# Order edges at the up-projection and in attention of a hybrid decoder block

## The chip, the cores and the metric

The kernel runs on one NeuronCore of a Trainium2 chip. The metric is the device time of one execution in microseconds; a time stated for a kernel is the median of its runs. TensorE (PE in the profile) multiplies matrices, VectorE (DVE), ScalarE (ACT) and GpSimd (POOL) work element by element, and SyncE (SP) issues most of the transfers. Each engine works through its own list of instructions in order.

## The reference

One decoder layer on `x` of 2048 tokens by 1024 channels, all in float32:

```python
h = rmsnorm(x, attn_norm);  z = h @ w_in          # pool | q | k | v | gate_pool | gate_attn
a = pool_mixer(u_pool, w_pool, pool_scale)        # 4 groups, causal means over 2, 4, 8, 16 tokens, minus u
q, k = rope(rmsnorm(q)) / 8, rope(rmsnorm(k))     # 16 query heads, 2 key heads of 64
b = sliding_window_attention(q, k, v, sinks)      # window 128, blocks of 128
x = x + (sigmoid(g_pool) * a + sigmoid(g_attn) * b) @ w_out
h = rmsnorm(x, ffn_norm)
up = causal_depthwise_conv(h @ w_up)              # width 3, 2 x 2816 channels
x = x + (silu(gate) * val) @ w_down
```

## The kernel before

Tokens go through in two chunks of 1024 (c = 0 and 1), channels on the partitions. Every float32 matrix product is made of three matmuls: each operand is split into a high part (a cast on ScalarE) and a low part (a subtraction on VectorE), and high x high, high x low and low x high are added up in PSUM. `split` (L249, L250), `halved` (L362, L363), `parted` (L1068, L1069) and `Down.make` (L1870, L1871) all do this: ScalarE's cast first, then VectorE's subtraction, and TensorE needs both.

A chunk has these stages. First the keys and values of eight blocks of 128 tokens, with query projections, and in chunk 0 the folding of `w_pool` into `w_in`, as fillers in between (`mixer`, first loop; L1939). Chunk 0 also takes its row norms here: `squares` (L683) sums the squares of one block of rows, which it loads first into a tile `M`, `norm1` makes the scale, `spread` (L666) turns it by transposes on TensorE.

Then attention, 32 items of four heads and one block (`mixer`, second loop; L1984). An item's `scores` makes the products, the masked maximum, the exponentials (L917) and the normalisation (L923); the next turn's `probabilities` transposes (L931), splits and masks (L939, on GpSimd) and `values` (L959) multiplies by the values. Between the items stand fillers: projections for queries, gates and pooled channels. What a filler leaves for the other engines is put in two lists. `later` holds the next slab's split, the gates' combination and the start of a pooling window; `run_later` empties it at every call. `slow` holds a window's doublings (L1015) and its end (`finish`: L1026, L1027, the store of `dd`); `run_later(n)` takes up to n of them. A window of 2, 4, 8 or 16 has 1, 2, 3 or 4 doublings. In the last group of chunk 0 the loop also calls `w.step` of gate units, which split their weights piece by piece (`Blocks.first` to `fourth`).

Then the gates, the output projection (`out_proj` in chunk 0, `out_blocks` with seven products in chunk 1), the up-projection (`up`) and the down-projection (`Down`). The gates, chunk 1's output projection, the up- and the down-projection use Strassen's scheme in Winograd's form, seven products of half-size blocks where eight would do, with sums on VectorE before and after. In `up`, a unit f is one tile of gate and value channels; its products `one` to `seven` each run 12 matmuls (`product`, L1254) into one PSUM bank. `three` adds to the bank that `one` began, and `kept` (L1444) copies it away on ScalarE; then `five` adds to that same bank (L1470 takes its result), and then `seven` (L1478). `four` and `six` share another bank. The first three units are interleaved by hand while the right-hand sums T1 to T4 are being made (`right_t1` to `right_t4`).

In `out_blocks`, `final` adds the residual (`added`, L1320), squares the result on ScalarE (L1332, L1335) and adds the square to a running sum (L1339); `stats` turns the sums into row scales with matmuls against ones (L655).

In `Down`, each step of the seven products has its operand made up to five steps ahead (`AHEAD`); at `P2` the step first makes a difference in place (L1888).

The order on each engine isn't the program's order. A planner (the tile framework's scheduler) walks the program once at build time, keeps a list of instructions by priority (the order in which they are traced), and with its own table of costs picks for each engine the first that it thinks ready; it also hands out the buffers of each pool then (`U` 19, `M` 5, `F` 4, `R` 3, `Q` 6). On the chip the order is fixed. `tc.issue_after(ins)` adds an order edge, without a wait: what the block traces on the engine of `ins` is planned behind `ins`. On other engines it does nothing.

Of the kernel before, what the change touches and what calls it, by code (L numbers as in the profile page):

```python
# [21 lines left out]
ALU = mybir.AluOpType  # L22
# [200 lines left out]
def block_kernel(ctx: ExitStack, tc: tile.TileContext, x, xT, pos, vec, qkn, w_poolT, w_pool, w_q, w_kv,  # L223
# [753 lines left out]
    def run_later(n=2, after=None):  # L977
        while later:
            later.pop(0)()

        with tc.issue_after(after) if after else nullcontext():
            for _ in range(min(n, len(slow))):
                slow.pop(0)()

    def gate_attn(c, ct, n, hs, ta, st):
# [22 lines left out]
    def windows(c, ct, u, st):  # L1008
# [20 lines left out]

        slow.append(finish)  # L1030

    def gated(c, ct, n, hs, ta, st):
# [217 lines left out]
    def product(bank, a, b, first):  # L1250
        i = 0
        for k in range(4):
            for x, y in ((0, 0), (0, 1), (1, 0)):
                nc.tensor.matmul(bank, a[:, x, k, :], b[k // 2][:, y, k % 2, :],  # L1254
                                 start=(first and i == 0), stop=(i == 11),
                                 skip_group_check=True)
                i += 1

    class Out:


        def __init__(self, c):
            self.c, self.m, self.w, self.b, self.xs, self.raws = c, [], [], {}, {}, []
            self.accs = [[], []]

        def mix(self):
# [51 lines left out]
        def added(self, h, n, m, bank):  # L1318
            x = self.xs[h, n][:, m]
            V.scalar_tensor_tensor(x, bank, 0.5, x, op0=ALU.mult, op1=ALU.add)  # L1320

# [4 lines left out]
        def final(self, h, n, m, bank):  # L1326
            self.added(h, n, m, bank)
            x = self.xs[h, n][:, m]
# [4 lines left out]
            else:  # L1333
                sq = mp.tile([P, 512], F32, "M")
                A.square(sq, x)  # L1335
                if h == 1 - n == 0 and m == 3:
                    accs.append(sq)
                else:
                    V.tensor_add(accs[0], accs[0], sq)  # L1339
            A.dma_start(x2d[4 * h + m][:, n * 512:n * 512 + 512], x)  # L1340
# [5 lines left out]
    def out_blocks(ob):  # L1346
# [52 lines left out]

        def stats(n):  # L1400
            rstd(ob.accs[n], r2[:, 4 * n:4 * n + 4])

# [30 lines left out]
    class Up:  # L1433
# [5 lines left out]
        def mul(self, bank, x, y, first=False):  # L1439
            product(bank, self.w.w[x], self.b[y], first)  # L1440

# [57 lines left out]
        def gate(self, yg=None):  # L1499
# [3 lines left out]
            A.activation(t, yg, AF.Silu)  # L1503
            V.tensor_mul(t, t, self.yv)
            load(actd[self.f], t)

    def up(c, xg, b, norms, heads, dn):
# [36 lines left out]
        with tc.issue_after(last):  # L1544
            right_b22(xg, b)
        u0.five()
        with tc.issue_after(third):
            right_t4(xg, b, t2s)
        weights(2, 1)
        u0.six()  # L1550
        yg = u0.conv(0, u0.ug)
# [6 lines left out]
        for f in range(2, FT + 1):  # L1558
# [24 lines left out]
            weights(f + 1, 1)  # L1583
            old.six()
            if f < FT - 1:
# [208 lines left out]
    class Down:  # L1794
# [80 lines left out]
        def run(self, extra):  # L1875

            gives = []
            for i, (g, p, k) in enumerate(self.steps):
# [7 lines left out]
                if p == "P2":  # L1886
                    a = self.raw[g, 0, k]
                    V.tensor_sub(a[:, 0:4:2], a[:, 1:4:2], a[:, 0:4:2])  # L1888
                if k > 0 and gives:
# [41 lines left out]
    def mixer(c, hs, kvw):  # L1931
# [7 lines left out]
        for n in range(NB):  # L1939
# [4 lines left out]
            if c == 0 and n == 3:  # L1944
                make_h(0, 2, hs)
                for i in range(4, NB):
                    squares(0, i, row(0, i))
            pk = [raw(0), raw(1)] if n == 0 else pk[1:] + ([raw(n + 1)] if n + 1 < NB else [])
# [11 lines left out]
            for f in fills:  # L1960
                filler(*f, c, hs, ta, st)
            next(parts, None)
            if n > 1 or n == c == 1:
# [20 lines left out]
        for i in range(len(items)):  # L1984
# [18 lines left out]
            if group == 3:  # L2003
                if c == 0:
                    if n == 0:
                        older = []
                        stream.fetch(stream.used + 2)
                    for f, steps in enumerate(({1: 1, 2: 2, 3: 1, 4: 0, 5: 0}, {5: 1, 7: 1})):
                        if n in steps:
# [137 lines left out]
```

## Time and profile before

| what | value |
|---|---|
| median of 3 runs | 2384.95 us (2383.26 to 2388.49) |
| the profiled execution | 2385.3 us |
| its span, first to last instruction | 2383.6 us |
| TensorE busy | 2356.7 us, 99% |
| VectorE / ScalarE / GpSimd busy | 1906.5 / 1185.7 / 190.5 us |
| mean granted TensorE clock | 0.998 |

A row of the groups reads: line, engine, operation, result from operands by tile names, shape, count, then busy time, mean of one in ns, and the idle time of the engine ahead of them with what ended it. A row of the timeline reads: start, length, engine, line, operation, tiles, shape, count, and in brackets the idle time ahead of it with what ended it. A row of the windows reads: stretch, its length, then for each engine busy time and instructions, the granted clock, the share of DMA time and GB/s.

### The profile page before, as it was taken

The page shows a single profiled execution, that of the slowest core. Times are in us where ns is not written, and L with a number is a line of the kernel's source. Part 1 is how long each engine was busy: PE and PEld are TensorE (multiplying, and loading weights), DVE is VectorE, ACT ScalarE, POOL GpSimd, SP SyncE. Part 2 cuts the span into 40 slices and gives each one's busy share as a digit, 9 for nine tenths or more (in the row PEclk, how much of TensorE's full clock was granted, in tenths as well). Part 3 has the DMA queues.
Part 4 walks back from the last instruction along what each step waited for, and adds up shares of the span by engine and source line. Part 5 has one row for each costly group of instructions (what it writes and reads, how often), then busy time and mean ns, then how long its engine had stood idle before and what let it go on. Part 6 is the DMA issues. An engine that isn't in the chain of part 4 may idle for free.

```text
span 2383.6 us, 30120 instructions
## 1 busy us (share of the span) xinstructions
PE 2356.7 (99%) x11040; PEld 1958.7 (82%) x11040; DVE 1906.5 (80%) x2907; ACT 1185.7 (50%) x2164; POOL 190.5 (8%) x142
## 2 busy tenths in 40 slices
PE   9999999999999999999999999999999999999999
PEld 8888888888788888888888888888788888888887
DVE  8688888977977777899955867788798777779994
ACT  7555455455654555643623544455445545554441
POOL 1123121010000000000002232200000000000000
PEclk9999999999999999999999999999999999999999
DMA  9768778697222233644454776666733222228421
GB/s 348 241 202 237 223 213 286 216 344 270 73 88 91 93 106 106 210 168 162 133 195 151 228 219 196 197 207 230 234 129 105 80 80 80 80 75 288 141 71 53
DMA packets 165060, 408.10 MB, mean 171 GB/s; under 512 B 14128, under 2 KB 50480, under 8 KB 155184
## 3 DMA queue, kind: packets, MB, share of 16 engines
q1 hardware_dynamic: 151616, 373.48, 46.6%
q0 software_dynamic: 8256, 24.12, 4.3%
q10 hardware_dynamic: 5040, 8.58, 1.0%
q8 instruction: 87, 1.43, 0.2%
q14 instruction: 61, 0.50, 0.1%
HBM read 267.32 MB, written 138.81 MB: 170 GB/s over the span
## 4 chain that ended last, share of the span: by engine, by line
PE 85%; DVE 8%; DMA 3%; ACT 2%; issue 1%; POOL 0%; SPq 0%; DVEq 0%; ACTq 0%; POOLq 0%
PE f L1254 22%; PE f L266 16%; PE t L1254 12%; PE a L1254 6%; PE f L1912 4%; PE a L1912 4%; PE s L1912 4%; PE t L1912 4%; PE f L1098 3%; PE a L959 2%; PE s L898 2%; PE a L266 2%; PE t L931 1%; DVE U L1069 1%; DMA U<-xd 1%
## 5 line engine op out<-in xcount | busy, mean ns | idle before, releaser
L266 PE MATMUL f<-U,U 128*128 128x512 f32 (+1 forms) x2088 | 490.2, 389 | 4.5 <-ACT U L249 2.1
L266 PEld LDWEIGHTS f<-U,U 128*128 128x128 f32 x2088 | 381.3, 189 | 81.3 <-ACT U L249 2.7
L1254 PE MATMUL f<-U,U 128*128 128x512 f32 x1872 | 445.1, 390 | 2.7 <-ACT Q L1444 2.5
L1254 PEld LDWEIGHTS f<-U,U 128*128 128x128 f32 x1872 | 350.8, 188 | 77.7 <-ACT Q L1444 3.8
L1492 DVE SCALAR_TENSOR_TENSOR M<-F,vc,M 128x1024 f32<-128x1024 f32 x176 | 225.3, 1282 | 139.0 <-ACT M L1489 138.7
L1254 PE MATMUL t<-U,U 128*128 128x512 f32 x1332 | 314.6, 389 | 0.0
L1254 PEld LDWEIGHTS t<-U,U 128*128 128x128 f32 x1332 | 249.7, 188 | 52.4 <-ACT Q L1444 0.3
L362 ACT CAST U<-R 128x1024 fp32r<-128x1024 f32 x147 | 153.6, 1053 | 82.0 <-DVE R L391 42.6
L1254 PE MATMUL a<-U,U 128*128 128x512 f32 x756 | 183.9, 390 | 0.7 <-ACT Q L1444 0.7
L363 DVE TENSOR_TENSOR U<-R,U 128x1024 fp32r<-128x1024 f32 x147 | 179.2, 1221 | 0.3 <-ACT U L362 0.3
L1254 PEld LDWEIGHTS a<-U,U 128*128 128x128 f32 x756 | 141.3, 188 | 30.2 <-ACT Q L1444 1.2
L1254 PE MATMUL f<-U,M 128*128 128x512 f32 x624 | 150.2, 389 | 0.3 <-DVE F L1470 0.3
L917 ACT ACTIVATE Q<-s,st,rq 128x128 f32<-128x128 f32 x256 | 113.8, 456 | 49.9 <-DVE st L914 49.7
L1254 PEld LDWEIGHTS f<-U,M 128*128 128x128 f32 x624 | 117.0, 188 | 25.0 <-DVE F L1470 0.8
L939 POOL TENSOR_SCALAR_AFFINE_SELECT M<-M 128x1024 fp32r<-128x1024 f32 x64 | 94.4, 1475 | 383.4 <-DVE st L919 230.4
L1870 ACT CAST U<-U 128x1024 fp32r<-128x1024 f32 x76 | 79.0, 1051 | 84.7 <-PE s L1912 22.2
L1478 ACT COPY F<-f 128x512 f32<-128x512 f32 x52 | 30.5, 586 | 182.2 <-PE f L1254 182.0
L1489 ACT ACTIVATE M<-F,vc 128x1024 f32<-128x1024 f32 x88 | 109.4, 1243 | 3.3 <-DVE F L1474 1.9
L1871 DVE TENSOR_TENSOR U<-U,U 128x1024 fp32r<-128x1024 f32 x76 | 92.0, 1219 | 2.7 <-ACT U L1870 2.5
L1870 ACT CAST F<-U 128x1024 fp32r<-128x1024 f32 x44 | 46.2, 1049 | 93.8 <-PE a L1912 62.5
L966 ACT COPY U<-a 128x512 f32<-128x512 f32 x64 | 37.5, 586 | 108.5 <-PE a L959 108.3
L1098 PE MATMUL f<-U,U 128*128 128x512 f32 x384 | 88.5, 390 | 0.3 <-DVE M L1104 0.2
(320 smaller groups left out, 4051.9 us busy)
## 6 DMA issues: line engine op xcount, KB each, us to landing
R<-w_up SPq DMA_DIRECT2D x80, 512.0 KB, 3.7
actd<-M SPq DMA_DIRECT2D x44, 512.0 KB, 2.7
U<-w_down SPq DMA_DIRECT2D x88, 256.0 KB, 5.0
U<-actd SPq DMA_DIRECT2D x88, 256.0 KB, 5.2
qd<-U SPq DMA_DIRECT2D x64, 256.0 KB, 3.8
Q<-qd SPq DMA_DIRECT2D x64, 256.0 KB, 4.7
R<-w_out SPq DMA_DIRECT2D x30, 512.0 KB, 4.5
U<-kept_S SPq DMA_DIRECT2D x12, 1024.0 KB, 7.9
```

Of the source, the lines that this page charges most:

```text
L266: nc.tensor.matmul(out, a, b, start=(i == 0), stop=(i == n - 1))
L362: A.copy(t[:, 0], raw)
L363: V.tensor_sub(t[:, 1], raw, t[:, 0].bitcast(F32))
L917: A.activation(pr[:, h, :], sc[:, h, 0:P], AF.Exp, bias=nm[:, h:h + 1], scale=it["rq"][:, h:h + 1], accum_out=rs[:, h:h + 1])
L939: G.affine_select(own.rearrange("p a h q -> p (a h) q"), pa.bitcast(F32).rearrange("p a h q -> p (a h) q"), pattern=[[0, 8], [1, P]], base ...
L1098: nc.tensor.matmul(po, w[:, a, k, :], ms[k // 2][n][:, b, k % 2, :], start=(first and i == 0), stop=(last and i + 1 == len(order)))
L1254: nc.tensor.matmul(bank, a[:, x, k, :], b[k // 2][:, y, k % 2, :], start=(first and i == 0), stop=(i == 11), skip_group_check=True)
L1489: A.activation(y, u[:, 2:], AF.Identity, bias=cw[:, 3, m:m + 1], scale=cw[:, 2, m:m + 1])
L1492: V.scalar_tensor_tensor(y, u[:, j:j + T], cw[:, j, m:m + 1], y, op0=ALU.mult, op1=ALU.add)
L1870: A.copy(hi, src)
L1871: V.tensor_sub(lo, src, hi.bitcast(F32))
L1912: nc.tensor.matmul(into[m], u[:, 0, c_], v[:, 1], start=(first and j == 0), stop=(k == n - 1 and j == 2), skip_group_check=True)
```

## The change

Nothing is added to or taken from what is computed; only order and edges change.

- `run_later(2)` takes one pooling step, not two, in a call by which a new window has been started (`fresh`) since the last such call.
- `product` returns its last matmul. In `up`, `u0.five` is planned behind the product traced before it (`u1.three`), `u0.six` behind `u0.five`, and `u1.six` (f = 2) behind `u0.six`. The weight step of unit 2 joins `right_t4` behind `third`, the last low part of T3, on VectorE.
- `final` puts the addition of a square to its sum in a list, and the next `final` traces it behind its own residual; `stats` empties the list.
- In `Down.run`, the difference of `P2` is planned behind the last product of gate and value (L1504).
- In `mixer`, chunk 0, block 3: the four `squares`, with the row loads they take, are traced behind that block's fillers.
- In the last attention group of chunk 0, third item, `run_later(0)` is called ahead of the weight steps.

```diff
@@ run_later
+        if n == 2 and run_later.fresh:
+            n, run_later.fresh = 1, False
         with tc.issue_after(after) if after else nullcontext():
             for _ in range(min(n, len(slow))):
                 slow.pop(0)()
+    run_later.fresh = False
@@ windows
         slow.append(finish)
+        run_later.fresh = True
@@ Out.final
-            self.added(h, n, m, bank)
+            with tc.issue_after(self.added(h, n, m, bank)):
+                while self.sums:
+                    self.sums.pop()()
...
-                    V.tensor_add(accs[0], accs[0], sq)
+                    self.sums.append(lambda: V.tensor_add(accs[0], accs[0], sq))
@@ out_blocks, stats
+            while ob.sums:
+                ob.sums.pop()()
@@ Up.mul, Up.gate
-            product(bank, self.w.w[x], self.b[y], first)
+            Up.end = product(bank, self.w.w[x], self.b[y], first)
...
-            V.tensor_mul(t, t, self.yv)
+            Up.gated = V.tensor_mul(t, t, self.yv).ins
@@ up
-        u0.five()
+        with tc.issue_after(Up.end):
+            u0.five()
         with tc.issue_after(third):
             right_t4(xg, b, t2s)
-        weights(2, 1)
-        u0.six()
+            weights(2, 1)
+        with tc.issue_after(Up.end):
+            u0.six()
+        six = Up.end
...
-            old.six()
+            with tc.issue_after(six) if f == 2 else nullcontext():
+                old.six()
@@ Down.run
-                    V.tensor_sub(a[:, 0:4:2], a[:, 1:4:2], a[:, 0:4:2])
+                    with tc.issue_after(Up.gated):
+                        V.tensor_sub(a[:, 0:4:2], a[:, 1:4:2], a[:, 0:4:2])
@@ mixer
                 make_h(0, 2, hs)
-                for i in range(4, NB):
-                    squares(0, i, row(0, i))
...
             for f in fills:
                 filler(*f, c, hs, ta, st)
+            if c == 0 and n == 3:
+                for i in range(4, NB):
+                    squares(0, i, row(0, i))
...
                         stream.fetch(stream.used + 2)
+                    if n == 2:
+                        run_later(0)
```

More of the change, by code (lines that the diff above doesn't have):

```diff
@@ L1253, in product @@
             for x, y in ((0, 0), (0, 1), (1, 0)):
-                nc.tensor.matmul(bank, a[:, x, k, :], b[k // 2][:, y, k % 2, :],
-                                 start=(first and i == 0), stop=(i == 11),
-                                 skip_group_check=True)
+                ins = nc.tensor.matmul(bank, a[:, x, k, :], b[k // 2][:, y, k % 2, :],
+                                       start=(first and i == 0), stop=(i == 11),
+                                       skip_group_check=True).ins
                 i += 1
+        return ins
     class Out:
@@ L1264, in __init__ @@
             self.accs = [[], []]
+            self.sums = []
         def mix(self):
@@ L1319, in added @@
             x = self.xs[h, n][:, m]
-            V.scalar_tensor_tensor(x, bank, 0.5, x, op0=ALU.mult, op1=ALU.add)
+            return V.scalar_tensor_tensor(x, bank, 0.5, x, op0=ALU.mult, op1=ALU.add).ins
         def residual(self, h, n):
```

## The prediction

> **What bounds the kernel now.** I read the page first, then what TensorE waited for, then the timeline at each of those waits, then windows for the granted clock. From the page: the busy line, one costly group and one DMA row.
>
> ```profile
> PE 2356.7 (99%) x11040; PEld 1958.7 (82%) x11040; DVE 1906.5 (80%) x2907; ACT 1185.7 (50%) x2164; POOL 190.5 (8%) x142
> L1254 PE MATMUL f<-U,U 128*128 128x512 f32 x1872 | 445.1, 390 | 2.7 <-ACT Q L1444 2.5
> U<-kept_S SPq DMA_DIRECT2D x12, 1024.0 KB, 7.9
> ```
>
> TensorE is busy 2356.7 of the span of 2383.6 us, and no edit removes or adds a matmul. Only the 26.9 us outside can be won, plus time lost to a lower clock. Who ended TensorE's waits (total us, times, longest):
>
> ```profile
> PE t L931 <- DVE Q L923: 4.1, 5, 1.4
> PE f L266 <- ACT U L249: 3.8, 5, 1.8
> PE f L1254 <- ACT Q L1444: 2.5, 2, 1.3
> PE a L655 <- DVE F L1339: 2.2, 1, 2.2
> ```
>
> These four rows are 12.6 of the 26.9 us, and each leads to lines that the diff reorders. Windows, with columns stretch, TensorE, weight loads, VectorE, ScalarE, GpSimd, clock, DMA:
>
> ```profile
> 353.50:357.10 3.60, 3.25 (x8) 2.61 (x9) 3.60 (x9) 2.20 (x10) 1.23 (x1) 0.53 0.83 261
> 608.20:611.80 3.60, 3.60 (x16) 2.97 (x17) 3.60 (x4) 2.90 (x3) 0.00 (x0) 1.00 0.02 5
> 1725.70:1729.20 3.50, 3.50 (x11) 2.61 (x10) 1.72 (x3) 0.63 (x1) 0.34 (x1) 0.51 0.97 298
> 1020.00:1080.00 60.00, 60.00 (x263) 49.14 (x263) 59.05 (x82) 24.90 (x30) 0.00 (x0) 1.00 0.47 161
> ```
>
> At full clock a matmul takes 3.60 / 16 = 0.225 us. At clock 0.53, eight took 3.25: 3.25 - 8 x 0.225 = 1.45 us lost, over and above the wait before them. The stretch at 1725.70, at 0.51, is as long, and I price it the same. The profile draws a matmul 0.39 us long but the next follows after 0.225, so each wait shown hides 0.16 more: a wait of w costs w + 0.16.
>
> **The up-projection's order (b).** Both chunks; first the weights' load and the waits in chunk 0, then in chunk 1:
>
> ```profile
> 595.74 0.32 SPq L243 DMA_DIRECT2D U<-kept_S  x1
> 607.56 0.58 ACT L1444 COPY Q<-f 128x512 f32<-128x512 f32 x1
> 608.20 3.04 PE L1254 MATMUL f<-U,U 128*128 128x512 f32 x12 [1.27 <-ACT Q L1444]
> 611.75 2.88 PE L1254 MATMUL f<-U,U 128*128 128x512 f32 x12
> 1760.58 0.32 SPq L243 DMA_DIRECT2D U<-kept_S  x1
> 1772.80 3.04 PE L1254 MATMUL f<-U,U 128*128 128x512 f32 x12 [1.27 <-ACT Q L1444]
> ```
>
> The product at 608.20 is `u0.five`: it accumulates into the bank that `kept` (L1444) is still copying, and TensorE stands still 1.27 us. `u1.three`, in another bank, was planned later, at 611.75. The new edge puts `u1.three` first: its 12 x 0.225 = 2.7 us of product cover the copy. Gain 1.27 + 0.16 = 1.43 a chunk, 2.9 in two. The cover fails if u1's weights S3/S2 are late, and `u0.five` is now queued behind them: each us late is a us lost. Issued at 595.74 with the median 7.9 us to landing they are there by 603.6, 3 us early; at 1760.58, 1768.5 against 1771.5. The edges on `u0.six` and `u1.six` keep products whole and cost nothing: the same matmuls follow. The weight step moved behind `third` delays VectorE work for unit 2 by about one subtraction; TensorE has units 0 and 1 in front of it. Bounds: 2.9 if both waits go, 1.4 if only one does. I take 2.9.
>
> **Sums behind the next residual (a).** Chunk 1's output projection:
>
> ```profile
> 1716.34 0.69 DVE L382 TENSOR_TENSOR R<-R,R 128x512 f32<-128x512 f32 x1 [4.71 <-DMA R<-w_up]
> 1717.26 4.24 PE L1298 MATMUL f<-U,U 128*128 128x512 f32 x18
> 1718.93 0.69 DVE L1339 TENSOR_TENSOR F<-F,M 128x512 f32<-128x512 f32 x1 [0.70 <-ACT M L1335]
> 1722.91 0.69 DVE L1339 TENSOR_TENSOR F<-F,M 128x512 f32<-128x512 f32 x1 [0.69 <-ACT M L1335]
> 1723.66 0.49 PE L655 MATMUL a<-one,F 128*128 128x1 f32 x3 [2.16 <-DVE F L1339]
> ```
>
> VectorE lost 4.71 us to the load of w_up, then ran residual, wait for ScalarE's square (0.70), sum, in rounds of (1722.91 - 1718.93) / 2 = 1.99. Without the wait a round is 1.29, or 0.645 an operation. After the change the sum of block m stands behind the residual of block m+1, when its square is long done. From 1716.34 + 0.65 come four residuals and four sums without idling, 8 x 0.645 = 5.2, ending at 1722.2; the fourth residual needs the first product of the row at 1717.26, done by 1717.26 + 2.7 = 1720.0, before its turn. So L655 starts at 1722.2, not 1723.66: 1.5 gained, and a wait of 0.7 stays. That is below the 1.27 of (b), after which the clock was 1.00 (row 608.20), so the 1.45 lost at 1725.70 goes too: 2.9. Bounds: 0.5 if the planner pulls another operation in between and the clock still drops; 2.16 + 0.16 + 1.45 = 3.8 if the wait vanishes. I take 2.9, by the counted operations. The sums hold their `M` tiles one block longer; the tile of block 3 of the first quarter is held through two products, with five `M` buffers, two of them temporaries. I cost that at nothing; the range of (a) covers it.
>
> **The split ahead of the weight steps (c).** Chunk 0, last attention group:
>
> ```profile
> 323.88 0.32 SPq L243 DMA_DIRECT2D R<-wfold  x1
> 349.03 0.69 ACT L1041 ACTIVATE F<-f,vc 128x512 f32<-128x512 f32 x1 [2.60 <-DVE f L1040]
> 350.22 1.04 ACT L362 CAST U<-R 128x1024 fp32r<-128x1024 f32 x1
> 351.17 1.14 ACT L249 CAST U<-R 128x512 fp32r<-128x512 f32 x2
> 351.84 1.19 PE L266 MATMUL f<-U,U 128*128 128x512 f32 x4 [1.79 <-ACT U L249]
> 353.85 6.74 PE L266 MATMUL f<-U,U 128*128 128x512 f32 x22 [0.51 <-DVE U L250]
> ```
>
> The next filler's slab was fetched at 323.88, yet its split (L249, L250) stands behind the weight step's cast (L362), and ScalarE idled 2.60 us before 349.03. `run_later(0)` traces the split first. If it fits into that idle stretch, both waits go with the clock drop: 1.79 + 0.16 + 0.51 + 0.16 + 1.45 = 4.1. If it only passes L362, it gains 1.04 and the clock may still drop: 1.0. The slab had 27 us to arrive, so I take 4.0. What is late instead are the steps of unit 0's weights, needed two fillers later.
>
> **Pooling steps one at a time (e).** Chunk 1's first item, then a collision in chunk 0:
>
> ```profile
> 1300.12 2.50 DVE L1015 TENSOR_TENSOR F<-F 128x1038 f32<-128x1038 f32 x2
> 1306.15 1.22 DVE L1015 TENSOR_TENSOR F<-F 128x1024 f32<-128x1024 f32 x1
> 1309.01 0.63 PE L931 MATMUL t<-identr,Q 128*128 128x128 f32 x4 [1.34 <-DVE Q L923]
> 336.63 2.10 POOL L939 TENSOR_SCALAR_AFFINE_SELECT M<-M 128x1024 fp32r<-128x1024 f32 x1 [5.97 <-DVE st L919]
> 337.69 2.11 DVE L1027 SCALAR_TENSOR_TENSOR F<-F,F 128x1024 f32<-128x1024 f32 x1
> ```
>
> With one doubling at 1300.12 instead of two the softmax chain behind it starts 1.25 earlier; the later slot holds as many as before. Of 1.34 I expect 1.0 back. At the four other waits of that row the doubling only changes its slot. Doublings, finish and the store of `dd` move one slot later; there are 28 steps a chunk against 32 slots of two, so none reaches the next stage. Bounds: all 4.1 of the row, and three new waits of its mean, 4.1 / 5 = 0.82, -2.5. I take 1.0. The last two rows speak against it: the finish took 2.11 beside a select of 2.10. The Trainium skill says why, in "SBUF — State Buffer", "Who interferes with whom": VectorE with two SBUF operands and a GpSimd instruction that reads SBUF lock each other out for a whole instruction. The trace agrees; by it a moved step that lands on a select makes both late, and (e) would be a loss.
>
> **Squares behind the fillers (f).** Chunk 0, block 3:
>
> ```profile
> 67.24 1.06 ACT L683 ACTIVATE M<-M 128x1024 f32<-128x1024 f32 x1
> 67.40 1.23 PE L266 MATMUL f<-M,U 128*128 128x256 f32 x6 [0.71 <-ACT U L249]
> 68.20 0.77 SPq L243 DMA_DIRECT2D M<-x  x1
> 68.30 0.61 ACT L249 CAST U<-R 128x512 fp32r<-128x512 f32 x1
> 73.68 1.06 ACT L683 ACTIVATE M<-M 128x1024 f32<-128x1024 f32 x1 [1.20 <-DMA M<-x]
> ```
>
> A square sits between the two casts that TensorE waits for: 0.71 + 0.16 can go, I take 0.8 and 1.2 at most, with the next cast. The moved step also issues four 512 KB row loads on SP, now planned behind the fillers' loads, and the fourth needs an `M` tile that a square frees. With the first square after the cast of 68.30 it is issued at 68.30 + 0.61 + 1.06 = 70.0, not 68.20; block 4's norm, and the transposes queued on TensorE, come 1.8 late: at worst 1.8 + 1.45 = -3.3. Query products stand ahead of them, which is why I take 0.8.
>
> **The difference at the down-projection (d).**
>
> ```profile
> 999.58 1.22 DVE L1888 TENSOR_TENSOR U<-U 128x1024 f32<-128x1024 f32 x1
> 1001.45 3.01 PE L1254 MATMUL f<-U,M 128*128 128x512 f32 x12 [0.35 <-DVE F L1470]
> ```
>
> L1888 stood in front of L1470; behind the last gate product it no longer does: 0.35 + 0.16 = 0.5. VectorE then has it in a stretch where it is busy 59.05 of 60 (row 1020.00), with operands made five steps ahead as cover; at worst as much is lost, -0.5.
>
> **Sum.** 2.9 + 2.9 + 4.0 + 1.0 + 0.8 + 0.5 = 12.1. Every edit also shifts the planner's list behind it; I allow one new wait of 0.82 a chunk, 1.6. That leaves 10.5. The profiled execution took 2385.3, 0.35 above the median of 2384.95: 2374.8 on its scale, 2374.5 as a median. All upper bounds, with no new wait, give 16.6 (2368.3); all lower ones, less the 1.6, give -5.0 (2390).
>
> **Rivals.** About 0.2%, 4.8 us, is what can be told from no change: 2380.2 to 2389.7.
> - *Waits change place.* Only (b), with fixed products, pays; (a), (c), (e) and (f) come back as waits on other lines, since the planner orders by its own costs: 2384.95 - 2.9 = 2382. For it: VectorE is 80% busy. Against: (c)'s operands were ready 27 us early.
> - *The clock does not come back.* The gaps shrink but the half-clock stretches stay: 2374.5 + 2 x 1.45 = 2377.4. Against: they follow exactly on the waits of 1.79 and 2.16, and none follows on the 1.27 of (b). (The Trainium skill, "TensorE: Matmul & The Clock Gate", "Why this matters for your kernels", lets the clock fall only for gaps over about 3 us; by that these waits would not be the cause. The trace, at 0.53 after 1.79 and 0.51, disagrees.)
> - *Slower: pooling steps on selects.* Each of the 32 attention items of a chunk has one select. A doubling or finish that meets it takes 2.11 - 1.22 = 0.9 longer, right ahead of L923, for which L931 waits. It decides from about 12 items (10.5 / 0.9); at 20 of them the time is 2374.5 + 18 = 2392.5. Now 5 of 64 wait, so this needs four times as many.
> - *More.* All five waits of L931 go and the allowance is not used: 2374.5 - 3.1 - 1.6 = 2369.8.
> - *The edges bind nothing*, because the planner already had this order: excluded by the rows 608.20 and 611.75.
>
> **Chances.** Forecast 0.60, waits change place 0.18, clock 0.06, more 0.10, slower 0.06. Faster by over 0.2%: 0.60 + 0.06 + 0.10 = 0.76, and 0.02 of the second case: 0.78. Within: 0.16. Slower: 0.06. The forecast's own range is 2371 to 2379; the one for 8 in 10 is 2368.5 to 2384, which reaches to the second case.
>
> **What would show it.** Right: no wait of L1254 on L1444 in `u0.five`; L655 waiting under 1 us and clock 1.00 behind it; L249 ahead of L362 and clock 1.00 around 350; L1888 behind the last L1504. Wrong: more than five waits of L931 on L923; a wait of `u1.three` on kept_S; a transposition L666 near 77 that waits for L683 or a row; a new window at half clock.

## Result: 18.7 us slower

The changed kernel takes 2403.19 us (median of 6 runs, 2401.17 to 2406.88) against 2384.46 for the kernel before beside it (6 runs, 2380.28 to 2388.49): the ratio is 1.0083, with a 95% interval of 1.0071 to 1.0095. The forecast was 2374.5, and its range ended at 2384.

The profiled execution took 2406.88 us, one of the two longest of the six, with a span of 2405.2. Line numbers of the changed kernel are a few higher: `product` is L1259, `kept` L1455, the sum behind `five` L1481, the cast and subtraction of `parted` L1073 and L1074, the residual L1327, the sum of squares L1348. The busy line of its page:

```profile
PE 2364.6 (98%) x11040; PEld 1963.7 (82%) x11040; DVE 1908.6 (79%) x2907; ACT 1185.5 (49%) x2164; POOL 199.7 (8%) x142
```

The counts are those of before (11040, 2907, 2164, 142): only order has changed. TensorE's busy time is 7.9 us longer, and 40.6 us of the span lie outside it, where it was 26.9. What ended TensorE's waits, the rows that bear on the change:

```profile
PE f L1259 <- DVE F L1481: 10.0, 4, 4.7
PE a L959 <- ACT M L933: 4.3, 1, 4.3
PE a L959 <- POOL M L939: 3.3, 4, 1.3
PE a L655 <- DVE F L1348: 2.0, 1, 2.0
PE t L931 <- DVE Q L923: 0.9, 2, 0.6
```

The waits that the prediction wanted gone are smaller (L923 was 4.1) or have other instances. New ones stand above them: the first row did not exist before beyond one wait of 0.35. The windows, cut where the clock changed (last columns: clock, DMA, GB/s):

```profile
86.43:89.84 3.41, 3.41 (x17) 3.41 (x17) 3.41 (x15) 0.79 (x2) 0.00 (x0) 0.50 0.06 26
393.63:397.04 3.41, 2.85 (x7) 2.25 (x8) 2.58 (x4) 3.41 (x5) 1.09 (x1) 0.50 1.02 404
632.56:639.38 6.82, 6.04 (x14) 4.79 (x15) 4.49 (x4) 4.87 (x8) 0.00 (x0) 0.50 0.00 0
1758.96:1765.78 6.82, 6.82 (x24) 5.95 (x24) 2.47 (x5) 1.26 (x3) 1.01 (x1) 0.50 0.89 310
1806.74:1810.16 3.42, 3.08 (x7) 2.51 (x8) 2.11 (x3) 3.36 (x4) 0.00 (x0) 0.50 0.00 0
```

Five stretches at half clock, 23.9 us in all, where before had two of 3.41. At a granted clock of 0.50 TensorE loses half of the time it works, so I estimate that a stretch of 3.41 or 6.82 us costs up to 1.7 or 3.4.

Where the time went, by stage. A stage ends where TensorE starts the first product of the next one; the numbers are differences from the profile of before, in us, and the stages left out differ by 0.03 at most. The last two columns are the experiments that split the change in two.

| stage | before | changed | `only_up` | `no_up` |
|---|---|---|---|---|
| start, keys and values, chunk 0 | 124.28 | +4.15 | +0.81 | +5.10 |
| attention, gates, output projection, chunk 0 | 455.15 | +0.89 | -0.37 | +2.81 |
| up-projection, chunk 0 | 424.87 | +7.99 | +9.52 | -0.71 |
| down-projection, chunk 0 | 212.61 | -1.19 | 0.00 | -1.18 |
| attention, chunk 1 | 263.95 | +1.19 | +1.79 | +1.41 |
| output and up-projection, chunk 1 | 505.25 | +8.12 | +0.72 | -3.94 |
| down-projection, chunk 1 | 211.27 | +0.53 | 0.00 | +0.54 |
| span | 2383.59 | +21.57 | +12.43 | +3.95 |

**How far such a table can be read.** One profile is one execution. Where an experiment leaves a stage's order as it was, the start came out between -0.1 and +1.6, attention to output projection of chunk 0 between -1.3 and +1.3, the up-projection of chunk 0 between -0.1 and +0.2, attention of chunk 1 between -0.2 and +0.3 but twice at +1.8 and +3.5, and output and up-projection of chunk 1 between -2.2 and +2.1. Nearly all of the last is the output projection (82.3 before): with VectorE's order there as before it took 77.9 to 84.4 in six kernels. From `up_fixed`:

```profile
1713.12 0.69 DVE L382 TENSOR_TENSOR R<-R,R 128x512 f32<-128x512 f32 x1 [0.40 <-DMA R<-w_up]
```

The load of `w_up`, for which VectorE waited 4.71 before, let it wait 0.40 in the profile of `up_fixed`, whose output projection has neither (a) nor another order on VectorE; it took 77.9, 4.3 less than before, and L655 did not wait. So a profile's gain of up to 4 us there can be the load's. The causes of the spread that I can see are transfers that land at another time, and whether a wait costs the clock. I call nothing an effect that lies within these ranges, and the medians decide.

### The profile page after: what moved, and what is told of

Read it like the earlier page. It is cut to its first block, busy times and chain, and to the rows that moved or that the text cites. A ratio compares the mean times of both kernels' runs of the same rounds, so it can differ in the third digit from the quotient of the medians.

```text
span 2405.2 us, 30132 instructions
## 1 busy us (share of the span) xinstructions
PE 2364.6 (98%) x11040; PEld 1963.7 (82%) x11040; DVE 1908.6 (79%) x2907; ACT 1185.5 (49%) x2164; POOL 199.7 (8%) x142
## 4 chain that ended last, share of the span: by engine, by line
PE 84%; DVE 8%; DMA 4%; ACT 2%; issue 1%; POOL 0%; DVEq 0%; SPq 0%; ACTq 0%; POOLq 0%
PE f L1259 21%; PE f L266 15%; PE t L1259 12%; PE a L1259 6%; PE f L1928 4%; PE a L1928 4%; PE s L1928 4%; PE t L1928 4%; PE f L1103 3%; PE a L959 2%; PE s L898 2%; PE a L266 2%; DMA tad<-U 1%; DVE U L1074 1%; DMA U<-xT 1%
## 5 line engine op out<-in xcount | busy, mean ns | idle before, releaser
L1259 PE MATMUL f<-U,U 128*128 128x512 f32 x1872 | 447.1, 391 | 2.3 <-ACT Q L1455 2.3
L1259 PEld LDWEIGHTS f<-U,U 128*128 128x128 f32 x1872 | 353.1, 189 | 77.7 <-ACT Q L1455 3.8
L1259 PE MATMUL t<-U,U 128*128 128x512 f32 x1332 | 315.1, 390 | 0.1
L1259 PEld LDWEIGHTS t<-U,U 128*128 128x128 f32 x1332 | 250.1, 188 | 53.1 <-DVE U L363 0.6
L1259 PE MATMUL a<-U,U 128*128 128x512 f32 x756 | 183.5, 391 | 0.7 <-ACT Q L1455 0.7
L1259 PEld LDWEIGHTS a<-U,U 128*128 128x128 f32 x756 | 141.3, 188 | 30.3 <-ACT Q L1455 1.2
L1259 PE MATMUL f<-U,M 128*128 128x512 f32 x624 | 154.5, 397 | 10.0 <-DVE F L1481 10.0
L1259 PEld LDWEIGHTS f<-U,M 128*128 128x128 f32 x624 | 119.5, 192 | 36.7 <-DVE F L1481 11.7
L939 POOL TENSOR_SCALAR_AFFINE_SELECT M<-M 128x1024 fp32r<-128x1024 f32 x64 | 100.4, 1569 | 380.1 <-DVE st L919 207.7
```

The source lines that it names most:

```text
L939: G.affine_select(own.rearrange("p a h q -> p (a h) q"), pa.bitcast(F32).rearrange("p a h q -> p (a h) q"), pattern=[[0, 8], [1, P]], base ...
L1259: ins = nc.tensor.matmul(bank, a[:, x, k, :], b[k // 2][:, y, k % 2, :], start=(first and i == 0), stop=(i == 11), skip_group_check=True).ins
```

## Experiments

Times are medians, with the median of before from the same group of runs on the same chip.

| kernel | median | before | ratio (95%) |
|---|---|---|---|
| changed | 2403.19 | 2384.46 | 1.0083 (1.0071 to 1.0095) |
| `only_up` | 2398.15 | 2384.09 | 1.0062 (1.0047 to 1.0077) |
| `no_up` | 2388.80 | 2384.09 | 1.0018 (1.0008 to 1.0027) |
| `five_rows` | 2397.11 | 2384.09 | 1.0054 (1.0039 to 1.0069) |
| `rest_split` | 2386.03 | 2384.09 | 1.0005 (0.9995 to 1.0015) |
| `up_fixed` | 2387.43 | 2384.47 | 1.0010 (1.0001 to 1.0019) |
| `sums_down` | 2382.13 | 2384.47 | 0.9991 (0.9982 to 1.0000) |
| `pool_only` | 2393.59 | 2384.47 | 1.0039 (1.0025 to 1.0052) |
| `best` | 2382.52 | 2384.47 | 0.9994 (0.9985 to 1.0004) |
| `split_late` | 2380.25 | 2383.52 | 0.9991 (0.9981 to 1.0001) |
| `all_fixed` | 2381.63 | 2383.52 | 0.9995 (0.9987 to 1.0004) |
| `rows_early` | 2382.24 (one run) | 2383.52 | - |
| `split_plain` | 2384.21 | 2385.34 | 0.9997 (0.9988 to 1.0007) |

### The change in two: `only_up` and `no_up`

`only_up` is the kernel before with the diff's parts in `product`, `mul` and `up`; `no_up` is the changed kernel without them.

> The kernel before with the four edits at the up-projection alone (the product's returned instruction, five and six behind the product traced last, the weight step under the edge of T4, u1.six behind u0.six). Theory A (each edit costs in its own stage): the up-projection of chunk 0 is again 8.0 us longer (424.9 to 432.9), that of chunk 1 about 8 of its 11.9, every other stage within 0.3, time about 2400.5. Rival B (the planner's list is one chain, so costs cannot be given to edits): other stages move by over 1 us too, and the two up-projections differ from 8.

> The changed kernel with the four edits at the up-projection undone, all else as changed. Theory A: 21.6 us of span less about 16: start +4.2, attention +1.5 and +1.2, output projection of chunk 1 -3.8, up-projection of chunk 0 +-0.3, of chunk 1 +4 (the wait for the sums of the second half and the slow clock behind it), time about 2390. Rival B: the up-projection of chunk 1 keeps more than 6 of its 11.9, or other stages move by over 1 us.

By the medians the up-projection costs 14.1 and the rest 4.7; together 18.8, where the whole change costs 18.7. So the two parts add up, and three quarters of the loss are the up-projection's. By stages theory A held in chunk 0 (+9.52, -0.71), and not in chunk 1: there `only_up` loses 0.7, `no_up` gains 3.9, and the changed kernel loses 8.1. Divided where the up-projection starts, the output projection is 3.8 to 4.3 shorter in all three, so that gain is the same one each time and does not add up; the up-projection is 5.0 longer in `only_up`, 0.1 shorter in `no_up`, and 11.9 longer in the changed kernel. One reason for the rest is in this execution. Residual loads in the changed kernel, then in `no_up`:

```profile
1730.38 1.23 POOL L1323 DMA_DIRECT2D U<-xT  x1 [7.99 <-issue]
1743.91 0.69 DVE L1327 SCALAR_TENSOR_TENSOR U<-t,U 128x512 f32<-128x512 f32 x1 [3.71 <-DMA U<-xT]
```
```profile
1723.49 1.23 POOL L1322 DMA_DIRECT2D U<-xT  x1 [6.59 <-issue]
1734.56 0.69 DVE L1326 SCALAR_TENSOR_TENSOR U<-t,U 128x512 f32<-128x512 f32 x1
```

The last load was waited for until 13.5 us after its issue; in `no_up`, with the same order of VectorE there but for one weight step, the residual started 11.1 us after the issue without a wait. VectorE lost 3.71, the second half's sums came 2.05 late for TensorE (the row of L655 above), and 6.82 us at half clock followed (row 1758.96). The medians, which add up without it, suggest that this is not in every run; one profile of the changed kernel cannot show it.

### The up-projection: `five_rows`, `rest_split`, `up_fixed`

What happens there in the changed kernel, chunk 0, from the timeline:

```profile
608.76 8.63 PE L1259 MATMUL f<-U,U 128*128 128x512 f32 x36
619.67 1.05 ACT L1073 CAST U<-U 128x1024 fp32r<-128x1024 f32 x1 [3.49 <-DVE U L1252]
620.62 0.58 ACT L1455 COPY Q<-f 128x512 f32<-128x512 f32 x1
621.25 3.06 PE L1259 MATMUL f<-U,U 128*128 128x512 f32 x12 [1.14 <-ACT Q L1455]
623.10 1.23 DVE L363 TENSOR_TENSOR U<-R,U 128x1024 fp32r<-128x1024 f32 x1 [1.12 <-ACT U L362]
624.24 0.68 DVE L1481 TENSOR_TENSOR F<-f,Q 128x512 f32<-128x512 f32 x1
624.98 3.01 PE L1259 MATMUL f<-U,M 128*128 128x512 f32 x12 [0.67 <-DVE F L1481]
629.89 2.60 DVE L1503 SCALAR_TENSOR_TENSOR M<-F,vc,M 128x1024 f32<-128x1024 f32 x2
632.59 0.69 DVE L1481 TENSOR_TENSOR F<-f,Q 128x512 f32<-128x512 f32 x1
633.34 5.49 PE L1259 MATMUL f<-U,M 128*128 128x512 f32 x12 [4.67 <-DVE F L1481]
```

`u0.three`, `u1.three` and `u0.five` run as 36 matmuls without a wait: the forecast's cover worked. But the copy of `u1.three`'s bank stands on ScalarE behind the cast of T4's second half, for which ScalarE stood idle 3.49 us, and `u1.five` waits for it. The sum of `u0.five`, done at about 617, is taken at 624.24, behind T4 and a weight subtraction that itself waits for ScalarE; and that of `u1.five` at 632.59, behind two convolution steps. `seven` accumulates into the bank that each sum has to read first. Three waits, 6.5 us, and a double stretch at half clock, for one wait of 1.27.

Two kernels ask which edge does it. `five_rows` has this and, in the start, the moved squares:

```diff
-        u0.five()
+        with tc.issue_after(Up.end):
+            u0.five()
...
+            if c == 0 and n == 3:            # behind the fillers, not ahead of raw()
+                for i in range(4, NB):
+                    squares(0, i, row(0, i))
```

`rest_split` has `weights(2, 1)` under T4's edge, the edges on both `six` and, in attention, `run_later(0)` at n == 2.

> The kernel before with two edits in stages that do not touch: the edge on u0.five alone at the up-projection, and the squares behind the fillers in chunk 0. Theory A1 (u0.five planned after u1.three ends later by the planner's costs, so its sum on VectorE falls behind T4's second half and unit 2's weight step): both up-projections 6 to 8 us longer with this edge alone, start +4.2, time about 2403. Rival A2 (the weight step moved under T4's edge, or the edges on six, do the damage): up-projections gain 1.4 to 2.9 each, time about 2385.

> The kernel before with two edits in stages that do not touch: the weight step under T4's edge with the edges on u0.six and u1.six (no edge on u0.five), and the split ahead of the weight steps in chunk 0's last attention group. Theory A1: up-projections within 1 us of before; rival A2: 6 to 8 us longer each. For the split, theory C1 (the wait of 4.35 us near 390 belongs to the pooling steps): attention of chunk 0 is 4.0 us shorter, as first predicted, time about 2380.5; rival C2 (it belongs to the split, which pushes the weight steps into the last items): 0 to 2 us longer, time 2385 to 2387.

`five_rows`: the up-projection of chunk 0 is 5.45 longer, and that of chunk 1 3.5 (2.36 with the output projection). That is A1 in sign, smaller than its 6 to 8, and not by its mechanism:

```profile
613.09 0.55 PE L1254 MATMUL t<-U,U 128*128 128x512 f32 x1 [2.22 <-ACT U L1068]
615.19 1.22 PE L1254 MATMUL t<-U,U 128*128 128x512 f32 x2 [1.13 <-DVE U L1069]
616.21 7.54 PE L1254 MATMUL f<-U,U 128*128 128x512 f32 x24
```

Here the planner drew single matmuls of `u0.six` ahead of the products, and they wait for B22's casts and subtractions, 2.22 and 1.13 us. So the edges on `six` are not neutral: without them this loss takes the place of the other. `rest_split`: +0.78 in chunk 0's up-projection, and -3.97 in output and up-projection of chunk 1. There VectorE has the weight step that waited 4.71 us for `w_up` no longer among the sums but behind them, at 1783; it is the same wait that part (a) gets round. `u0.five`'s edge alone is harmful and the moved step with the edges on both `six` nearly harmless, so A2 falls; A1 has the right edge, but its time of 2403 was not reached (2397.1).

`up_fixed` keeps the edges on `five` and both `six`, moves no weight step, and adds:

```diff
@@ right_t4
         for j in range(2):
-            q21 = half(xg[j + 2], 0)
...
+            with behind(after if j else ()):
+                q21 = half(xg[j + 2], 0)
...
@@ five
-            V.tensor_add(self.uv[:, 514:], self.x, self.p5)
+            Up.added = V.tensor_add(self.uv[:, 514:], self.x, self.p5).ins
...
@@ up
-            right_t4(xg, b, t2s)
+            right_t4(xg, b, t2s, (Up.added, Up.last,))
```

`Up.added` is `u0.five`'s sum, `Up.last` the copy of `u1.three`'s bank.

> The kernel before with the edges on u0.five, u0.six and u1.six, and two more edges: the second half of right_t4 is planned behind u0.five's sum on VectorE and behind u1's copy (kept) on ScalarE. No weight step is moved. Theory V (the products' new order is sound, and the loss is that VectorE's and ScalarE's lists put u0.five's and u1.five's sums and u1's copy behind T4 and the weight steps): the waits of 1.2, 0.7 and 4.5 us of the changed order go, each up-projection is 0 to 1.4 us shorter than before, time 2381.3 to 2384. Rival W (any product order but the old one makes the later lists wait): each up-projection is still 3 us or more longer, time 2390 or more.

```profile
605.78 8.66 PE L1255 MATMUL f<-U,U 128*128 128x512 f32 x36
613.18 0.58 ACT L1446 COPY Q<-f 128x512 f32<-128x512 f32 x1
615.46 0.68 DVE L1472 TENSOR_TENSOR F<-f,Q 128x512 f32<-128x512 f32 x1
626.12 3.01 PE L1255 MATMUL f<-U,M 128*128 128x512 f32 x12 [0.35 <-DVE F L1472]
1788.22 3.02 PE L1255 MATMUL f<-U,M 128*128 128x512 f32 x12 [1.77 <-DVE F L1472]
```

The copy is taken at 613.18, ahead of T4's second half, and `u0.five`'s sum at 615.46, about 1 us behind its product; in chunk 0 one wait of 0.35 is left: the same 36 matmuls without a wait as in the changed kernel are now part of a stage 0.8 shorter than before instead of 8.0 longer. Theory V holds there. Since the weight step also stays where it was, the run does not tell which of the two, T4's second half or that step, weighed more on VectorE. In chunk 1, 1.77 remain and the up-projection is 1.5 longer. The median, 2387.43 with runs from 2382.8 to 2389.4, missed theory V's 2381.3 to 2384: the loss fell from 14.1 to 3.0, and no gain came. The profiled execution, at 2383.89, is one of the fastest of the ten (the load of `w_up` above), so where the rest of the 3.0 goes is not shown.

### The start: `rows_early`

In the changed kernel:

```profile
71.96 1.93 SPq L243 DMA_DIRECT2D M<-x  x2
77.96 1.06 ACT L683 ACTIVATE M<-M 128x1024 f32<-128x1024 f32 x1 [5.93 <-DMA M<-x]
79.68 1.06 ACT L683 ACTIVATE M<-M 128x1024 f32<-128x1024 f32 x1 [0.56 <-DMA M<-x]
82.70 0.66 PE L666 MATMUL s<-identr,M 128*128 128x128 f32 x4 [0.87 <-DVE M L664]
85.22 0.73 PE L266 MATMUL f<-U,U 128*128 128x512 f32 x2 [1.86 <-ACT U L832]
```

Two row loads, not one, are issued late, at 71.96 and just after, where the last was at 68.20. The transposes wait 0.87, the next product 1.86, and a stretch at half clock follows (row 86.43). All three kernels with this edit have it: +4.15, +5.10, +5.24.

```diff
-                for i in range(4, NB):
-                    squares(0, i, row(0, i))
+                late = [row(0, i) for i in range(4, NB)]
...
+            if c == 0 and n == 3:            # behind the fillers
+                for i in range(4, NB):
+                    squares(0, i, late[i - 4])
```

> The kernel before with the squares of chunk 0's block 3 behind the fillers, as in the change, but the row loads still ahead of the fillers. Theory M (the 4.4 us of the start come from the row loads, issued at 55.78 to 72.70 instead of 52.92 to 68.20, the last two waiting for M tiles that squares free): the loads are issued as before, no wait at L666, start within 0.8 us of before. Rival (the squares themselves are too late on ScalarE, whenever the rows arrive): start 3 us or more longer.

```profile
68.17 0.81 SPq L243 DMA_DIRECT2D M<-x  x1
77.32 0.60 PE L666 MATMUL s<-identr,M 128*128 128x128 f32 x4
```

The last load is back at 68.17, the transposes at 77.32 do not wait, and the start is 0.9 shorter than before, a little below the -0.1 to +1.6 of unchanged starts. Theory M holds in this one run: the loads made the loss, not the squares.

### Attention: `pool_only`, `split_late`, `split_plain`

In the changed kernel the waits at 351.84 and 353.85 are gone, and near 390 stands this:

```profile
380.67 1.02 POOL L971 DMA_DIRECT2D tad<-U  x1 [2.50 <-DMA tad<-U]
392.58 0.58 ACT L966 COPY U<-a 128x512 f32<-128x512 f32 x1 [3.93 <-DMA tad<-U]
394.19 0.80 PE L959 MATMUL a<-M,U 128*128 128x512 f32 x1 [4.35 <-ACT M L933]
```

The copy of item 4's values got a `U` buffer that the second store of `tad` was still reading, 11.9 us after its issue. On ScalarE it stands ahead of the cast for which TensorE waits. `rest_split`, with the split alone, has the same wait:

```profile
378.25 1.02 POOL L971 DMA_DIRECT2D tad<-U  x1 [2.49 <-DMA tad<-U]
389.88 0.59 ACT L966 COPY U<-a 128x512 f32<-128x512 f32 x1 [3.39 <-DMA tad<-U]
```

TensorE waits 3.59 us for the cast behind it. Attention to output projection of chunk 0 is 2.4 longer; C2 held for the time, and C1 fell. `pool_only` has the `fresh` lines of `run_later` and nothing else.

> The kernel before with one pooling step instead of two behind a new window, nothing else. First prediction: the wait of L931 at 1309 and others go, 1.0 us shorter. By the changed kernel's stages: attention of chunk 1 is 1.2 us longer (new waits for GpSimd's selects), and in chunk 0 it is -1.0 (the changed kernel's +1.5 less the +2.4 of the split alone): time 2384.3, no change. Rival (the steps meet selects on VectorE and GpSimd): 3 us or more longer.

It costs 9.1 us, the size that the rival had, and meets the same wait by itself, with the copy 11.7 us behind the store's issue:

```profile
392.41 1.52 PE L959 MATMUL a<-M,U 128*128 128x512 f32 x2 [3.67 <-ACT M L933]
```

Its stages: +5.4 in chunk 0's attention to output projection, +1.0 in chunk 1's attention, where the three kernels with this edit all have +1.0 to +1.4, and 1.7 in output and up-projection of chunk 1, which is within the spread named above. My sum of +0.0 had treated the wait near 390 as the split's alone; either edit makes it, and together they pay it once. `split_late` joins the split, part (a) and part (d), and moves the copy behind the cast:

```diff
+        if c == 0 and it["q4"] == 0 and n == 4:
+            held.append(lambda: A.copy(t[:, :, n % 4 * P:n % 4 * P + P], pv))
+        else:
+            A.copy(t[:, :, n % 4 * P:n % 4 * P + P], pv)
...
+        with tc.issue_after(cast):           # in probabilities, behind the cast L933
+            for f in held:
+                f()
```

> The kernel before with the split ahead of the weight steps, the sums behind the next residual and the difference behind the last gate product; and one more edit: in chunk 0's last group the copy of the values of item 4 (L966) into its U tile is traced and planned behind the next cast of the probabilities (L933). Theory U (with the split or the pooling steps moved, the planner hands that copy a U buffer that the second store of tad, on GpSimd's queue, still reads, 11 to 12 us from issue to landing, and puts the copy ahead of the cast for which TensorE waits 3.6 us): the wait near 390 falls below 1 us, attention of chunk 0 is 3 to 4 us shorter than before, with the gains of the other two edits (4.3 in the stages, 2.3 by the medians) 2377 to 2379. Rival (the split makes VectorE or ScalarE late there whatever the buffer): the wait stays over 2 us, time 2382 to 2385.

```profile
389.23 0.59 ACT L973 COPY U<-a 128x512 f32<-128x512 f32 x1 [2.53 <-issue]
389.87 0.50 PE L965 MATMUL a<-M,U 128*128 128x512 f32 x1 [2.72 <-ACT U L973]
```

The cast is early now, at 386.10, but TensorE waits for the copy itself: the next values go to the PSUM bank that it empties. The copy again starts 11.7 us behind the store's issue, though the profile names no releaser here. The expectation of under 1 us failed, and the stage is 1.0 longer, not 3 to 4 shorter; the order on ScalarE was not the cause. `split_plain` asks after the store:

```diff
+            if c == 0 and key == (0, 0):
+                load(tad2, t[64:P])          # a plain store elsewhere; the sum is left out
+            else:
+                G.dma_start(dst, t[64:P], accum_op=ALU.add)
```

> The kernel before with the split ahead of the weight steps alone, and for the first four blocks of chunk 0's last group the second half of the values is stored by a plain transfer on SyncE to a place of its own, where it was added onto tad by a transfer of GpSimd's queue; so that part of the attention's sum is left out of the result. All other work and the order of ScalarE's list around 390 (the copy L966 of item 4 ahead of the cast L933) stay. Theory U (the copy waits for a U buffer that the slow second store still reads, 11 to 12 us from issue to landing, and holds the cast or the PSUM bank): the wait near 390 falls below 1 us and attention of chunk 0 is 3 to 4.5 us shorter than before, which the split alone had 2.4 us longer; time about 2380.5. Rival (the split itself makes ScalarE or VectorE late there): the wait stays over 2 us and the stage is 0 us shorter or longer.

```profile
376.75 0.63 SPq L243 DMA_DIRECT2D tad<-U  x1
387.71 0.60 ACT L968 COPY U<-a 128x512 f32<-128x512 f32 x1
```

No wait is left at the copy, which stands ahead of the cast as in `rest_split`: the plain store went out 1.5 us earlier than the adding one (row 378.25 there, since it need not wait for the first) and had let go of the tile within 11.0. Attention to output projection of chunk 0 is 2.1 shorter than before, 4.5 less than with the same split and the slow store. Theory U holds for the wait. The 3 to 4.5 us did not come whole: waits of 0.8 for a select at 356 and 0.9 for the exponentials at 386 stand there. Nor did the time of 2380.5: the median is 1.1 below before, and its interval holds 1.

### Together: `sums_down`, `best`, `all_fixed`

`sums_down` is parts (a) and (d) alone; `best` is `sums_down` with `up_fixed`; `all_fixed` is `split_late` with `up_fixed` and an edge that plans `u0.value`, its convolution and a weight step behind `u1.five`'s sum.

> The kernel before with the sums behind the next residual in chunk 1's output projection and the difference of P2 behind the last gate product, nothing else. Theory A (costs stay in their stages): chunk 1's output projection and up-projection together 3.9 us shorter, the down-projections 0.6 shorter in sum, time 2379.6. Rival B: a gain below 1 us, because the wait for the sums comes back for the second half (2.05 us and a slow clock in the changed kernel's profile): time 2383 to 2386.

> up_fixed and sums_down in one kernel. By theories V and A the two add up: the stages' gains are 0 to 2.8 and 4.5 us, time 2376.8 to 2379.6, faster than before. Rival: the weight load of VectorE's wait in chunk 1 (4.71 us before) moves on into the up-projection once the sums no longer wait, and the sum of gains is below 2 us: 2382 or more.

> split_late and up_fixed together, and one more edge at the up-projection: what is traced behind u1.five up to the gate of u0 (the copies of conv, the weight steps) is planned behind u1.five's sum on VectorE. Theory V for chunk 1 (the 1.77 us that were left in up_fixed are u1.five's sum behind three weight subtractions and two convolution steps): that wait falls below 0.5 us, both up-projections are 1 to 1.5 us shorter than before, time 2 to 3 us below split_late. Rival (VectorE is full there, another operation is late in its stead): the up-projections are as in split_late or longer.

`sums_down`: output and up-projection of chunk 1 are 3.1 shorter, no wait at L655 in either half, the down-projections 0.5 shorter in sum; by the median 2.3 faster, with an interval that ends at 1.0000. VectorE waited 3.37 for `w_up` here, and L655 did not wait:

```profile
1715.26 0.69 DVE L382 TENSOR_TENSOR R<-R,R 128x512 f32<-128x512 f32 x1 [3.37 <-DMA R<-w_up]
```

So A held in its mechanism and B's wait did not come; but 2382.13 lies between A's 2379.6 and B's 2383. `best` and `all_fixed` are no faster than `sums_down`, and `best` came out at its rival's time: chunk 0's up-projection is 1.5 shorter in both, chunk 1's 3.0 and 1.4 longer. In `all_fixed`:

```profile
1778.77 2.60 DVE L1508 SCALAR_TENSOR_TENSOR M<-F,vc,M 128x1024 f32<-128x1024 f32 x2 [0.86 <-ACT M L1505]
1781.48 0.69 DVE L1486 TENSOR_TENSOR F<-f,Q 128x512 f32<-128x512 f32 x1
1782.23 3.01 PE L1264 MATMUL f<-U,M 128*128 128x512 f32 x12 [2.36 <-DVE F L1486]
```

The weight steps have gone from ahead of `u1.five`'s sum, two convolution steps stand there instead, and the wait grew from 1.77 to 2.36: theory V for chunk 1 fell, its rival held. What would make chunk 1 as good as chunk 0 stays open. `split_late` has the lowest median, 3.3 below before, and its interval still touches 1: none of these versions is shown to be clearly faster than the kernel before.

## Why the prediction was wrong, step by step

**(b), forecast 2.9 won, measured 14.1 lost.** The step that failed is the bounds, "2.9 if both waits go, 1.4 if only one does": they price the moved product by TensorE's list alone and put what it does to VectorE's and ScalarE's lists at nothing, as does "cost nothing: the same matmuls follow". I followed TensorE's list and the weights' arrival, and both came out as I wrote. What I left out is that a product's order carries its sum on VectorE and its copy on ScalarE along, and that operations which themselves wait stand ahead of them then (the cast at 619.67 after 3.49 us, the subtraction at 623.10 after 1.12). I take it that the product planned later made its sum later by the planner's clock; no run shows the planner's reckoning. `up_fixed` shows the cost: with two edges on those lists, and the weight step left in its place, chunk 0 is 0.8 shorter instead of 8.0 longer. In the profile of before the sum stood 1.0 us behind its product (608.20 + 3.04), between the halves of T4:

```profile
612.24 0.68 DVE L1470 TENSOR_TENSOR F<-f,Q 128x512 f32<-128x512 f32 x1
613.97 1.22 DVE L1247 TENSOR_TENSOR U<-U,M 128x1024 f32<-128x1024 f32 x1
```

That place was what `u0.seven` lived on, and the prediction speaks of L1470 only at the down-projection. A loss belonged in the bounds; no row excluded it.

**(f), forecast 0.8 won, measured about 4.2 lost** (4.8 on the mean of three kernels, less 0.6, the mean of nine unchanged starts). The mechanism stands in the prediction with its rows and a price of -3.3, and I took the other end, "Query products stand ahead of them, which is why I take 0.8". They did not reach: 48 matmuls at 0.225, 10.8 us, from 70.64 to 81.45, against rows that landed in time for squares at 77.96 and 79.68. I also counted one late load; two wait for tiles that squares free.

**(c), forecast 4.0 won, measured 2.4 lost alone in its stage** (1.9 by the median of `rest_split`, with the moved step beside it). The two waits and their clock stretch went, as worked out. The failed step is "What is late instead are the steps of unit 0's weights": late was a copy 37 us further on. The split takes its `U` tile before the weight step now, and the tiles after it, as I read it, get other buffers: the profile names the store that the copy waits for, not the buffers. With the store changed the stage is 2.1 shorter, about half of the forecast, which the median does not show.

**(e), forecast 1.0 won, measured 9.1 lost alone.** L931's waits on L923 fell from 4.1 to 0.9, more than forecast. But selects (L939) now end 3.3 us of waits, where they ended 0.6; chunk 1 loses 1.0 to 1.4, and in chunk 0 the edit alone runs into the same store, with 6.83 us at half clock behind the wait: 5.4 in that stage. The failed step is the lower bound, "three new waits of its mean", -2.5: the wait that came was 3.67 alone, and the clock went with it. The slower rival had the selects, at 0.9 an item; four waits, not twenty.

**(a), forecast 2.9 won: right in its mechanism, its size open.** The first half's L655 does not wait at all in the six kernels that have the edit, with up to 3.4 us of waiting for `w_up` ahead; without it, it waits 1.2 to 2.2 in the five profiles where `w_up` is waited for 3.8 us or more. The stage is 3.1 to 3.9 shorter where (a) stands without the up-projection's edits, but `up_fixed`'s output projection was 4.3 shorter without (a). By the median (a) and (d) together give 2.3, with an interval from 0 to 4.3. `rest_split` got the 4.0 by the moved weight step, so in the whole change both edits take away one and the same wait.

**(d), forecast 0.5 won: the wait went as worked out.** In `sums_down` the product that waited 0.35 at 1001.45 stands so:

```profile
1001.04 2.88 PE L1254 MATMUL f<-U,M 128*128 128x512 f32 x12
```

It belongs to the up-projection of chunk 0, which is 0.7 shorter in the three kernels that have (d) and otherwise the order of before there. Another 0.6 came at the start of the down-projection, where a wait of 0.56 for L1478 went that I had not counted; chunk 1 gave nothing. (The rest of the 1.19 in the table, and the 0.53 lost in chunk 1, `pool_only` has too, with 0.65 and 0.46.)

**The allowance** of 1.6 for a shifted list was the wrong kind of term. Not one average wait a chunk came, but five specific ones of 1.9 to 4.7, each with half clock behind it. Of the rivals, "waits change place" was the right kind, and its 2382 wrong in size, because it still let (b) pay. Of the signs of being wrong, two came: half-clock windows, and L666 late behind a row (at 82.70, by way of the norm's L664); u1.three's wait on kept_S and more waits on L923 did not. The signs of being right came too, but for L655's wait in the second half: they looked at the waits that the change takes away, not at those that it could make.

## What to carry to other kernels

Where an order edge moves a product, list what the program traces with it on the other engines, and look in the profile where those operations stand and how full that list is; in chunk 0 the edge paid only when they were tied as well. Where an edit changes when a tile is first written, every later tile of that pool may get another buffer: look for the slowest transfer that reads one, and ask who would wait if that buffer became theirs. When a bound has a loss with a mechanism and rows, and the cover is only counted roughly, price it before choosing the side.

## What the runs showed of the hardware

**The clock is judged on a fixed grid.** In the fourteen profiles there are 28 stretches at half clock, the end of the program aside. All are 3.41 or 6.83 us long, and all begin at a whole multiple of 3.413 us from the first clock record. Whether a wait costs the clock depends on how it lies on that grid: 26 of the 28 followed a grid stretch in which TensorE stood still for 1.93 us or more in all, by the starts of its matmuls, each counted as 0.225 us, and two one of 1.1 and 1.5, in which many products were narrower (128x256 and 128x1). The other way round, of the stretches after which the clock stayed full, the one with the most idle time by this count had 2.0 us, the next 1.8. In `rest_split` a wait of 1.79 lay in one stretch and cost the clock of the next:

```profile
1463.86:1467.28 3.42, 1.63 (x12) 1.21 (x11) 3.04 (x9) 1.96 (x9) 2.03 (x1) 1.00 0.73 267
1467.28:1470.69 3.41, 3.41 (x12) 2.74 (x11) 3.25 (x6) 1.75 (x3) 0.00 (x0) 0.50 0.24 97
```

In `only_up` a wait of 3.17 ended at 1799.85, lay over two stretches (1.86 and 1.31), and cost nothing of the clock. So the prediction's split between waits of 1.27 and 1.79 was partly chance, and the price, by the clock of 0.50, is up to 1.71 a stretch of 3.41 us, where I had 1.45. The Trainium skill, "TensorE: Matmul & The Clock Gate", "What's actually happening", says that the activity window is 3413 ns long and runs freely, and the traces agree to the digit. It also gives the lower clock after a whole idle window; here 1.93 us of one were enough.

**A store holds its tile long.** In six kernels the copy near 390 started 11.5 to 12.0 us after the issue of the second store of `tad` (64 partitions, 512 KB). In three of them (the changed kernel, `no_up`, `rest_split`) the profile names the store as what the copy waited for, 3.4 to 4.2 us; in `pool_only`, `split_late` and `all_fixed` the delay is the same and no releaser is named. Moving the copy in ScalarE's list left TensorE a wait of 2.72 (`split_late`); changing the store left none there (`split_plain`).
